# A hybrid RG-LRU and Conformer block on one core: four dot products of a gate at another place in the queue, and a layer norm taken about a mean of seven tiles

## The chip, the cores and the metric

The kernel runs on one core of a Trainium2 chip. The metric is the device time of one execution in microseconds (us); several executions are timed and their median is given. A core has five engines that take their instructions from queues of their own, each strictly in its order: TensorE (PE, matmuls), VectorE (DVE), ScalarE (ACT), GpSimd (POOL) and SyncE (SP, which only starts transfers here). They wait for each other by semaphores.

## The reference, cut to what matters

Two layers, a latent stream of 1024 tokens by 1024 features. Each layer is a mixer and then a gated ConvFFN; each of the two is scaled and shifted by six vectors (shift, scale, gate, twice) that come from the conditioning vector `c`. What the change touches is the second gate `g2` of the first layer, and the layer norm inside the second layer's mixer.

```
s_c = silu(c)
mod = s_c @ ada_w[i] + ada_b[i]                      # 6 x 1024 values
sh1, sc1, g1, sh2, sc2, g2 = split(mod, 6)
...
def conv_ffn(xm, w_up, cw, cb, w_down, rows, width):
    u = dwconv2d(xm @ w_up, cw, cb, rows, width)     # 3x3 depthwise, 5632 channels
    v, g = split(u, 2)
    return (silu(g) * v) @ w_down
h = h + g2 * conv_ffn(xm2, ...)

def conformer_conv(xm, w1, b1, cw, cb, lng, lnb, w2, b2):
    u = xm @ w1 + b1
    a, g = split(u, 2)
    v = dwconv1d(a * sigmoid(g), cw, cb, (15, 15))   # 31 taps
    v = silu(layernorm(v, lng, lnb))
    return v @ w2 + b2
def layernorm(x, g, b):
    mu = mean(x); var = mean(square(x - mu))
    return (x - mu) * rsqrt(var + EPS) * g + b
```

## The kernel before, in words

Activations lie with features on the 128 partitions (8 tiles of 128 features) and tokens along the free dimension, in two halves of 512 tokens (half 0, half 1). Every large product is made of three fp32r products (high by high, low by high, high by low), for which weights and activations are split: ACT copies the high part, POOL or DVE subtracts it (`whi`, `wlo` for weights, `xmh`, `xml` for activations, `zh`, `zl` and `dnh`, `dnl` in the FFN). PE's accumulators are four tiles `P[0]` to `P[3]` of two banks each (the rows call them `ps`).

**Who sets the order.** The class `Order` keeps a clock of estimated durations. `o.pe(...)` puts a PE step at the place where the code stands; the steps of the other engines wait in a pool, and the one with the earliest possible start, then the lowest `prio`, then the oldest, is issued next. So `prio` and the estimated readiness set each engine's fixed queue; on the chip an engine takes its rows in that order and waits wherever a row isn't ready.

**The FFN of layer 0** (`ffn`, 22 pairs p). A pair makes two tiles of the up projection (`col_tile`, f = p and 22 + p), each in one of `P[0]`, `P[1]`, `P[2]` in turn. ACT and DVE make the 3x3 convolution of a tile from PSUM (`ffn_conv`: one ACT step, eight DVE steps, which are called taps below, into `cv`), ACT takes the SiLU, DVE multiplies (`cv<-cv,cv`), and ACT and POOL split the product (`zh`, `zl`). From pair 3 on, `between()` puts a step of the down projection (`unit`) after every fourth k-step: 12 matmuls into `P[3]`, then on DVE `h<-ps,mod,h`, which multiplies by the gate `g2` and adds to the residual. The next unit needs `P[3]` free again.

**The gate's dots.** `g2` of layer 0 is eight columns of `mod` (q = 40 to 47), each a dot of a 128x1024 weight tile with `sC` (silu(c) on all partitions) by `ada_dot`: four on DVE (`raw,mod<-raw,sC`), made in `first_tiles` of pair 0 with `prio=3`, then four on POOL (`raw<-raw,sC`) with the sum on ACT (`raw,mod<-raw`). The tiles are loaded into a ring of two buffers, `raw_76` and `raw_77`, which the down projection's weights (`down_in`) share. `ada_bias(0, 5)` adds the bias to the eight columns (`mod<-mod,vec`); every `h` step needs it.

**The Conformer** (`conformer`). The 31-tap convolution of tiles 0, 2, 4, 6 is done on DVE (`taps`, into `CV`), that of tiles 1, 3, 5, 7 on PE (`conv`, 36 steps of three 256-column matmuls each into `P[3]`, four groups j of nine shifts). After a PE tile DVE copies its two halves to `yt`, two transfers write them to DRAM (`cdr<-yt`), four read them back rearranged (`sC<-cdr`), and ACT adds the bias (`CV<-sC,vec`). Tile 7 is the last. POOL has meanwhile summed tiles 0 to 4 into `lna` (`nacc`).

**The layer norm before.** `center(0)` multiplies `lna` and tiles 5, 6, 7 by a matrix of 1/1024 (`ones`), which gives the mean on all partitions; DVE subtracts it from eight tiles (`CV<-CV,ps`), ACT squares each, PE sums the squares with `ones` into `P[1]`, ACT and DVE make the reciprocal root (`rs`). `src` then feeds the second product (`k_outer`, 8 steps k per half): for each tile DVE multiplies by `rs`, ACT takes SiLU and the high part, DVE the low part (`xml<-CV,xmh`). In step k=0 PE also makes the mean of half 1 (`center(1)`), and in step k=3 it makes half 1's variance (`deviation`) from the sum of squares that DVE and POOL add up in turn (`nacc<-nacc,tt`).

Of the kernel before, what the change touches and what calls it, by code (L numbers as in the profile page):

```python
# [13 lines left out]
AF = mybir.ActivationFunctionType  # L14
ALU = mybir.AluOpType
ADD, SUB, MULT = ALU.add, ALU.subtract, ALU.mult
# [5 lines left out]
ND = D // P  # L22
# [258 lines left out]
class Net:  # L281
# [115 lines left out]
    def split(self, raw, rawB, slot, eng="pool", n=1024, hi_eng="act"):  # L397
        hi, lo, hB, lB = slot
        if hi_eng == "act":
            self.act(n, hi, raw, AF.Copy, [rawB], [hB])  # L400
        else:
            self.o.op("dve", 0.1 + n * 0.00053, lambda: self.nc.vector.tensor_copy(hi, raw), [rawB], [hB])
        self.tten(n, lo, raw, hi.bitcast(F32), SUB, [rawB, hB], [lB], eng=eng)
# [136 lines left out]

    def ada_dot(self, l, q, eng="dve", after=(), prio=0):

        t, b = self.load_raw(self.a["ada"][l, q], after=() if prio else after)
        col, mB = self.mod[l][:, q:q + 1], self.modB[l][q // 8]
        if eng == "dve":
            self.stt(1024, t, t, 1.0, self.sC, MULT, MULT, [b, self.sCB], [b], [mB], accum=col, after=after, prio=prio)
        else:
            self.tten(1024, t, t, self.sC, MULT, [b, self.sCB], [b], eng=eng, prio=prio)  # L550
            self.act(1024, t, t, AF.Copy, [b], [b], [mB], accum=col)
# [511 lines left out]
    def ffn(self, l, end, last=None):  # L1063
        o = self.o
# [39 lines left out]
        def quarter(g, q):  # L1104
            quarters[g, q] = load_down(g, q * 256, 256, dn.next())
# [12 lines left out]
        def zsplit(p, a, aB):  # L1118
            zh, zl, zhB, zlB = zr.next()
            Z[p] = zh, zl, [[zhB, zlB]] * 2  # L1120
            self.act(1024, zh, a, AF.Copy, [aB], [zhB])
            self.tten(1024, zl, a, zh.bitcast(F32), SUB, [aB, zhB], [zlB], eng="pool")
# [16 lines left out]
        ada = [(0, q) for q in range(40, 48)] + [(1, q) for q in range(48)] if l == 0 else []  # L1139
# [4 lines left out]
        for p in range(NF):  # L1144
            if p >= 3 and p % 2 == 1 and p < NF - 1:
                g = (p - 3) // 2
                todo += [(g, q, d) for q in range(4) for d in (2 * q, 2 * q + 1)]
            pts, accs = [], []
            if ada and 0 < p < 3:
                for _ in range(2):  # L1150
                    self.ada_dot(*ada.pop(0), "pool", prio=3)
                if p == 2:
                    self.ada_bias(0, 5)
            for q in ((), (0,), (1, 2))[p] if p < 3 else ():
                quarter(0, q)
            if p == 0:
                self.first_tiles((0, 1), lambda ops: [self.ada_dot(*ada.pop(0), prio=3, after=ops) for _ in range(4)] if ada else None)
                pts, nt = [0, 1], 2
            for i, f in enumerate((p, NF + p)):
                if p:  # L1160
                    self.col_tile(self.w_next(), nt % 3, between)
                    pts.append(nt % 3)
                    nt += 1
                acc, accB = cv.next()
                accs.append((acc, accB))
                if f < 2 * NF - 1:
                    self.ffn_conv(l, f, pts[i], acc, accB)
            (a, aB), (gt, gB) = accs
            if p < NF - 1:
                self.act(1024, gt, gt, AF.Silu, [gB], [gB])  # L1170
                self.tten(1024, a, a, gt, MULT, [aB, gB], [aB])
                zsplit(p, a, aB)
            else:
                last_gate(2 * NF - 1, pts[1], a, aB, gt, gB)
            for _ in range(3 if p > 2 else 0):
                if ada:
                    self.ada_dot(*ada.pop(0), "pool", prio=3)

        if l == 0:
# [4 lines left out]
            m = self.mod[1][:, 16:24]  # L1184
# [24 lines left out]
    def conformer(self, pool):  # L1209
        nc, o = self.nc, self.o  # L1210
        W, HS = 1024, 4
        CV = pool.tile([P, ND, W], F32, name="CV")
        cvB = [[Buf(), Buf()] for _ in range(ND)]
# [10 lines left out]
        yt, yB = pool.tile([P, W], F32, name="yt"), [Buf(), Buf()]  # L1224
        yr, yrB = self.sC, Buf(after=[self.sCB])
        rs2 = [self.rs, (pool.tile([P, 512], F32, name="rs2"), Buf())]
        lna = self.acc
        LATE = (5, 6, 7)
# [4 lines left out]
        outB = [[Buf(), Buf()] for _ in range(ND)]  # L1233
# [32 lines left out]
        def glu(m, pt):  # L1266
# [12 lines left out]
            self.act(W, inner(hi), split(xr), AF.Copy, [xrB], [hB], prio=-2)  # L1279
            self.tten(W, inner(lo), split(xr), inner(hi).bitcast(F32), SUB, [xrB, hB], [lB], prio=-2)  # L1280

        def conv(m):
            hi, lo, hB, lB = xs[m // 2 % 2]
            out = self.P[3].rearrange("p a (b s) -> p (a b) s", b=2)
            slot = None
            for j in range(4):
                for n, d in enumerate(SHIFTS):
                    i = j * len(SHIFTS) + n
                    if i % 8 == 0:
                        slot = self.w_next()  # L1290
                    wh, wl, whB, wlB = slot
                    c, s = slice(i % 8 * P, i % 8 * P + P), slice(HS + d, HS + d + 256)

                    def go():
                        for q, (w, x) in enumerate(((wh, hi), (wh, lo), (wl, hi))):
                            self.mm(out[:, j, :], w[:, c], x[:, j, s], n == 0 and q == 0, n == len(SHIFTS) - 1 and q == 2)

                    o.pe(3 * (256 / 2400 + 0.011), go, [whB, wlB, hB, lB], [self.PB[3][j // 2]])
            for h in range(2):
                c = slice(512 * h, 512 * h + 512)  # L1300
                self.ts(512, yt[:, c], self.P[3][:, h, :], 1.0, None, MULT, None, [self.PB[3][h]], [yB[h]], prio=-2)
                self.dma(self.cdr[m][:, c], yt[:, c], 262144, r=[yB[h]], w=[outB[m][h]], prio=-2)
            src = self.cdr[m].rearrange("(o c) (j s) -> j c o s", o=4, j=4)
            yrB.begin()
            for j in range(4):
                self.dma(split(yr)[32 * j:32 * j + 32], src[j], 131072, r=[outB[m][j // 2]], wp=[yrB], prio=-2)

            for h in range(2):
                c = CV[:, m, h * 512:h * 512 + 512]
                self.act(  # L1310
                    512, c.rearrange("p (s i) -> p s i", i=4), split(yr)[:, :, 128 * h:128 * h + 128].rearrange("p i s -> p s i"),
                    AF.Identity, [yrB], [cvB[m][h]], bias=self.v("cf_conv_b", m), prio=-1,
                )
            summed(m)
# [18 lines left out]
        def center(h, bank, sums):  # L1333

            xs = [(CV[:, m, h * 512:h * 512 + 512], cvB[m][h]) for m in range(ND)]
            parts = [lna[h], *(xs[m] for m in LATE)]
            mu, muB = self.P[bank[0]][:, bank[1], :], self.PB[bank[0]][bank[1]]
            for i, (t, tB) in enumerate(parts):
                o.pe(0.87, lambda: self.mm(mu, self.ones, t, i == 0, i == len(LATE)), [self.onesB, tB], [muB])
            for x, b in xs:  # L1340
                self.tten(512, x, x, mu, SUB, [b, muB], [b], prio=3 * h - 2)
            for m in range(ND):
                sums(m, *xs[m])

        var = self.P[1][:, 0, :]

        def sums(m, x, b):
            sq, sqB = self.tt.next()
            self.act(512, sq, x, AF.Square, [b], [sqB])
            o.pe(0.87, lambda: self.mm(var, self.ones, sq, m == 0, m == ND - 1), [self.onesB, sqB], [self.PB[1][0]])  # L1350

        center(0, (0, 0), sums)
        self.rsqrt(512, rs2[0][0], var, [self.PB[1][0]], [rs2[0][1]])

        def deviation(bank):
            ms = self.stat(*lna[1], bank)
# [2 lines left out]
        first = {0: lambda bank: center(1, bank, lambda m, x, b: self.norm_add(m, 1, x, b, ("dve", "pool")[m % 2])), 3: deviation}  # L1359
# [4 lines left out]
        def src(hf, k):  # L1364
            while self.fed < min(hf * ND + k + 5, 16):
                h, m = order[self.fed]
                self.fed += 1
                c = slice(h * 512, h * 512 + 512)
                x, b = CV[:, m, c], cvB[m][h]
                self.tten(512, x, x, rs2[h][0], MULT, [b, rs2[h][1]], [b])  # L1370
                silu = self.act(512, x, x, AF.Silu, [b], [b], bias=self.v("cf_ln_b", m), scale=self.v("cf_ln_g", m))
                self.z_split(m, x, b, "dve")
                if self.fed == 16:
                    self.sqrt_soon([silu])
            return self.z_slot((hf * ND + k) % 8)
# [81 lines left out]
```

## Time and profile before

| | us |
|---|---|
| median of 3 runs | 2440.19 (2438.97 to 2441.34) |
| the profiled execution, its own time | 2438.16 |
| its span from the first to the last instruction | 2436.4 |
| PE busy | 2326.2 (95%) |
| DVE busy | 1896.6 (78%) |
| ACT busy | 967.3 (40%) |
| POOL busy | 798.1 (33%) |
| PE idle for others, longest single wait | 23.0 |

The share of an engine is an average over stages. What a place is worth is read from PE's idle time at that place and from what released PE there. A number in square brackets at the end of a row is the engine's idle time just before that row, with the instruction that ended it.

### The profile page before, as it was taken

Reading aid. Unit: us, or ns where it says so; the run is one execution under the profiler, and the core shown is the slowest. Engines: PE = TensorE matmul, PEld = TensorE weight load, DVE = VectorE, ACT = ScalarE, POOL = GpSimd, SP = SyncE. Lnnn points to the kernel's source line nnn. Section 1 sums busy time; section 2 is a strip of 40 time slices with the busy share of each in tenths; the row PEclk is TensorE's granted clock in tenths of the full one; section 3 lists DMA queues with packets and bytes.
Section 4 is the critical chain, followed back from the end, with each engine's and each line's share of the span. In section 5 each row is a group of like instructions: output and inputs, shape, how many; then the busy total and the mean of one; then the engine's idle time right before and its main releaser. Section 6 shows DMA issues by size and latency. Waiting matters only on the chain.

```text
span 2436.4 us, 26124 instructions
## 1 busy us (share of the span) xinstructions
PE 2326.2 (95%) x10440; PEld 1892.8 (78%) x10440; DVE 1896.6 (78%) x1752; ACT 967.3 (40%) x1141; POOL 798.1 (33%) x409
## 2 busy tenths in 40 slices
PE   7999999889789999999999999889999999999997
PEld 2788888667578888888887888667888888888886
DVE  6677877776867777777878898677997777777878
ACT  4577777544233333333324333365322221222223
POOL 1100000354345544554523233245333322332323
PEclk9999999899899999999999999899999999999999
DMA  6324325253132323223211233422111111111101
GB/s 262 120 84 144 94 84 162 96 198 117 55 101 95 104 87 104 95 88 103 91 35 36 66 114 105 138 70 91 52 58 52 44 39 52 52 52 48 44 26 70
DMA packets 82442, 214.98 MB, mean 88 GB/s; under 512 B 8528, under 2 KB 33104, under 8 KB 82192
## 3 DMA queue, kind: packets, MB, share of 16 engines
q1 hardware_dynamic: 80448, 210.68, 26.3%
q10 hardware_dynamic: 1872, 2.62, 0.3%
q8 instruction: 82, 1.34, 0.2%
q14 instruction: 40, 0.33, 0.0%
HBM read 192.10 MB, written 13.63 MB: 84 GB/s over the span
## 4 chain that ended last, share of the span: by engine, by line
PE 70%; DVE 16%; ACT 5%; issue 3%; DMA 2%; POOL 2%; SPq 0%; ACTq 0%; DVEq 0%; POOLq 0%
PE ps L441 70%; DVE cv L362 4%; DVE CV L362 3%; DVE F L770 1%; ACT F L354 1%; POOL wlo L369 1%; DVE F L362 1%; DVE tt L362 1%; DVE F L369 1%; DVE rs L384 1%; ACT tt L354 1%; DVE raw L362 1%; ACT L354 1%; DVE h L362 1%; ACT whi L354 1%
## 5 line engine op out<-in xcount | busy, mean ns | idle before, releaser
L362 DVE SCALAR_TENSOR_TENSOR cv<-ps,vec,cv 128x960 f32<-128x960 f32 (+2 forms) x720 | 861.5, 1198 | 203.6 <-ACT cv L354 185.2
L441 PE MATMUL ps<-xmh,whi 128*128 128x512 f32 x2272 | 744.5, 394 | 19.7 <-ACT xmh L354 8.9
L441 PE MATMUL ps<-xmh,wlo 128*128 128x512 f32 x2272 | 738.0, 392 | 9.5 <-POOL wlo L369 5.9
L441 PE MATMUL ps<-xml,whi 128*128 128x512 f32 x2272 | 740.5, 393 | 4.6 <-DVE xml L362 4.2
L369 POOL TENSOR_TENSOR wlo<-wraw,whi 128x1024 fp32r<-128x1024 f32 (+1 forms) x164 | 399.8, 2442 | 712.6 <-ACT whi L354 694.9
L441 PEld LDWEIGHTS ps<-xmh,whi 128*128 128x128 f32 x2272 | 427.8, 189 | 115.9 <-ACT xmh L354 12.0
L441 PEld LDWEIGHTS ps<-xmh,wlo 128*128 128x128 f32 x2272 | 429.4, 189 | 103.1 <-POOL wlo L369 7.9
L441 PEld LDWEIGHTS ps<-xml,whi 128*128 128x128 f32 x2272 | 429.8, 189 | 102.4 <-DVE xml L362 9.4
L362 DVE SCALAR_TENSOR_TENSOR h<-ps,mod,h 128x1024 f32<-128x1024 f32 (+2 forms) x216 | 231.5, 1080 | 61.0 <-PE ps L441 60.8
L354 ACT ACTIVATE whi<-wraw 128x1024 fp32r<-128x1024 f32 (+1 forms) x198 | 205.2, 1042 | 123.3 <-PE ps L441 51.5
L354 ACT ACTIVATE cv<-ps,vec 128x1024 f32<-128x1024 f32 (+1 forms) x90 | 105.9, 1181 | 299.5 <-PE ps L441 280.5
L369 POOL TENSOR_TENSOR zl<-cv,zh 128x1024 fp32r<-128x1024 f32 x42 | 101.2, 2411 | 350.6 <-ACT zh L354 350.6
L441 PE MATMUL ps<-zh,dnh 128*128 128x512 f32 x576 | 180.1, 393 | 23.0 <-DVE h L362 23.0
L369 POOL TENSOR_TENSOR raw<-raw,sC 128x1024 f32<-128x1024 f32 x52 | 125.1, 2406 | 178.7 <-DMA raw<-ada_in 174.0
L441 PE MATMUL ps<-zl,dnh 128*128 128x512 f32 x576 | 181.4, 397 | 0.0
L441 PE MATMUL ps<-zh,dnl 128*128 128x512 f32 x576 | 177.8, 390 | 0.0
L354 ACT ACTIVATE raw<-raw 128x1024 f32<-128x1024 f32 x52 | 55.2, 1062 | 289.4 <-POOL raw L369 289.4
L354 ACT ACTIVATE cv<-cv 128x1024 f32<-128x1024 f32 (+1 forms) x46 | 47.0, 1022 | 293.5 <-DVE cv L362 293.3
L369 POOL TENSOR_TENSOR dnl<-raw,dnh 128x512 fp32r<-128x512 f32 x72 | 94.0, 1307 | 202.5 <-ACT dnh L354 202.5
L362 DVE SCALAR_TENSOR_TENSOR CV<-ps,vec,CV 128x1009 f32<-128x1009 f32 (+14 forms) x120 | 153.1, 1275 | 8.6 <-ACT CV L354 4.9
L441 PEld LDWEIGHTS ps<-zh,dnh 128*128 128x128 f32 x576 | 108.6, 189 | 45.9 <-DVE h L362 23.4
L441 PEld LDWEIGHTS ps<-zh,dnl 128*128 128x128 f32 x576 | 108.4, 188 | 26.4
(141 smaller groups left out, 2414.6 us busy)
## 6 DMA issues: line engine op xcount, KB each, us to landing
raw<-ada_in SPq DMA_DIRECT2D x88, 512.0 KB, 4.2
wraw<-up_in SPq DMA_DIRECT2D x88, 512.0 KB, 3.3
raw<-down_in SPq DMA_DIRECT2D x72, 256.0 KB, 3.2
wraw<-w_in SPq DMA_DIRECT2D x32, 512.0 KB, 3.3
wraw<-w_in_in SPq DMA_DIRECT2D x20, 512.0 KB, 3.9
wraw<-w_out_in SPq DMA_DIRECT2D x20, 512.0 KB, 3.7
wraw<-cw_in SPq DMA_DIRECT2D x16, 512.0 KB, 3.6
wraw<-gw_in SPq DMA_DIRECT2D x10, 512.0 KB, 3.4
```

What stands on the lines that cost most here:

```text
L354: "act", 0.21 + n * 0.00083, lambda: self.nc.scalar.activation(out, in_, func, **kw),
L362: lambda: self.nc.vector.scalar_tensor_tensor(out=out, in0=in0, scalar=scalar, in1=in1, op0=op0, op1=op1, **kw),
L369: return self.o.op(eng, dur, lambda: e.tensor_tensor(out=out, in0=in0, in1=in1, op=op), r, w, wp, prio=prio)
L384: return self.o.op("dve", 0.07 + n * 0.0063, lambda: self.nc.vector.reciprocal(out=out, in_=in_), r, w)
L441: self.nc.tensor.matmul(out, w, x, start=start, stop=stop)
L770: lambda t=t, a=a, ig=ig, rev=rev: nc.vector.tensor_tensor_scan(rev(t), rev(a), rev(ig), 0.0, op0=MULT, op1=ADD),
```

## The change

It has two parts that don't touch each other. **First**, the four DVE dots of `g2` get priority 0 in place of 3, the same as the taps of the convolution. `early` keeps the load's old rule (it doesn't wait for `after`).

**Second**, half 0's layer norm. `provisional()` is called inside the last convolution tile, after the sixth shift of its last group, and multiplies `lna` and tiles 5 and 6 by `ones` into `P[0]`'s second bank: the sum of seven tiles over 1024. `deviate` subtracts 8/7 of it, which is the mean of the seven tiles, from each tile (one DVE step, PSUM and SBUF in) and squares it on ACT. Tiles 0 to 6 and their sums of squares no longer need tile 7. When tile 7 is there, its deviation goes to a buffer `w` (`raw_76`), one product of `w` with `ones` gives `mu`, the distance of the true mean from the provisional one (the seven tiles' deviations sum to nothing), the variance is the mean square less `mu` squared, and `d`, a copy of `mu` in SBUF, is subtracted from each tile before it is multiplied by `rs`.

```diff
-    def ada_dot(self, l, q, eng="dve", after=(), prio=0):
+    def ada_dot(self, l, q, eng="dve", after=(), prio=0, early=False):
-        t, b = self.load_raw(self.a["ada"][l, q], after=() if prio else after)
+        t, b = self.load_raw(self.a["ada"][l, q], after=() if early else after)
...
-                self.first_tiles((0, 1), lambda ops: [self.ada_dot(*ada.pop(0), prio=3, after=ops) for _ in range(4)] if ada else None)
+                self.first_tiles((0, 1), lambda ops: [self.ada_dot(*ada.pop(0), early=True, after=ops) for _ in range(4)] if ada else None)
...
+        def provisional():
+            parts = [lna[0], *((CV[:, m, :512], cvB[m][0]) for m in LATE[:-1])]
+            for i, (t, tB) in enumerate(parts):
+                o.pe(0.87, lambda: self.mm(self.P[0][:, 1, :], self.ones, t, i == 0, i == len(parts) - 1), [self.onesB, tB], [self.PB[0][1]])
...
+                    if m == ND - 1 and j == 3 and n == 5:
+                        provisional()
...
-        def sums(m, x, b):
-            sq, sqB = self.tt.next()
-            self.act(512, sq, x, AF.Square, [b], [sqB])
-            o.pe(0.87, lambda: self.mm(var, self.ones, sq, m == 0, m == ND - 1), [self.onesB, sqB], [self.PB[1][0]])
-        center(0, (0, 0), sums)
-        self.rsqrt(512, rs2[0][0], var, [self.PB[1][0]], [rs2[0][1]])
+        def deviate(m, y, yB):
+            self.stt(512, y, mp, -ND / (ND - 1.0), CV[:, m, :512], MULT, ADD, [cvB[m][0], mpB], [yB], prio=-3)
+            sq, sqB = self.tt.next()
+            self.act(512, sq, y, AF.Square, [yB], [sqB], prio=-4)
+            return sq, sqB
+        for m in range(ND - 1):
+            total(var, varB, *deviate(m, CV[:, m, :512], cvB[m][0]), m == 0, False)
+        w, wB = vt[:, :512], vB
+        sq = deviate(ND - 1, w, wB)
+        total(mu, muB, w, wB, True, True)
+        total(var, varB, *sq, False, True)
+        sq, sqB = self.tt.next()
+        self.act(512, sq, mu, AF.Square, [muB], [sqB], prio=-4)
+        self.act(512, d, mu, AF.Copy, [muB], [dB], prio=-3)
+        self.tten(512, r, var, sq, SUB, [varB, sqB], [rB], prio=-4)
+        self.rsqrt(512, r, r, [rB], [rB])
+        inverse = list(rB.w)
...
+                if h == 0:
+                    x, b = (w, wB) if m == ND - 1 else (x, b)
+                    o.op("dve", 0.72, lambda x=x: nc.vector.tensor_tensor(out=x, in0=x, in1=d, op=SUB), [b, dB], [b], after=inverse if m else ())
                 self.tten(512, x, x, rs2[h][0], MULT, [b, rs2[h][1]], [b])
```

DVE's queue at the start of layer 0's FFN, the place of the fourth dot (`raw_77,mod`; `cv_3479` is the convolution of pair 0's first tile):

```order
 L362 SCALAR_TENSOR_TENSOR raw_76,mod_92<-raw_76,sC 128x1024
 L362 SCALAR_TENSOR_TENSOR cv_3479<-ps_65,vec,cv_3479 128x960 x2
+L362 SCALAR_TENSOR_TENSOR raw_77,mod_92<-raw_77,sC 128x1024
 L362 SCALAR_TENSOR_TENSOR cv_3479<-ps_65,vec,cv_3479 128x16x63 x2
 L362 SCALAR_TENSOR_TENSOR cv_3479<-ps_65,vec,cv_3479 128x15x63 x4
```

The fourth dot has moved from behind the taps of pair 2's second tile (five tiles' taps later) to behind the second tap of the first tile; the bias step `mod<-mod,vec` now stands behind the second tap of pair 1's first tile (`cv_3481`), and the first `h` step behind the seventh tap of pair 2's first tile (`cv_3480`), where before it came after the dot and the bias.

PE's queue in the last convolution tile (`cxh`, `cxl`: its input, `whi_82`, `wlo_83`: its weights), the first and the last row of each piece of the difference:

```order
 L441 MATMUL ps_68<-cxl_7759,whi_82 128x256
 L441 MATMUL ps_68<-cxh_7758,wlo_83 128x256
+L441 MATMUL ps_65<-nacc_89,ones 128x512
+L441 MATMUL ps_65<-CV,ones 128x512 x2
 L441 MATMUL ps_68<-cxh_7758,whi_82 128x256
-L441 MATMUL ps_65<-nacc_89,ones 128x512
-L441 MATMUL ps_65<-CV,ones 128x512 x3
-L441 MATMUL ps_66<-tt,ones 128x512 x8
+L441 MATMUL ps_66<-tt,ones 128x512 x7
+L441 MATMUL ps_65<-raw_76,ones 128x512
+L441 MATMUL ps_66<-tt,ones 128x512
```

The mean's products have moved into the tile, three matmul steps of three ahead of its end; the squares of seven tiles, the product of `w` and the last square follow the tile.

DVE's queue from the copies of the last tile on, before (-) and now (+):

```order
-L377 TENSOR_SCALAR yt<-ps_68 128x512 x2
-L369 TENSOR_TENSOR CV<-CV,ps_65 128x512 x8
+L377 TENSOR_SCALAR yt<-ps_68 128x512
+L362 SCALAR_TENSOR_TENSOR CV<-ps_65,CV 128x512
+L377 TENSOR_SCALAR yt<-ps_68 128x512
+L362 SCALAR_TENSOR_TENSOR CV<-ps_65,CV 128x512 x6
+L362 SCALAR_TENSOR_TENSOR raw_76<-ps_65,CV 128x512
+L369 TENSOR_TENSOR rs<-ps_66,tt 128x512
+L1397 TENSOR_TENSOR CV<-CV,nacc_89 128x512
 L384 RECIPROCAL rs<-rs 128x512
```

A deviation stands between the two copies; the subtraction of `d` from tile 0 stands ahead of the reciprocal, and seven more of these (L1397, both inputs in SBUF) follow it, one ahead of each tile's product with `rs`. In ACT's queue the copy of a weight tile (`whi<-wraw`) stands between the last square and the square of `mu`.

## Rows read from the trace of the kernel before

**Rows 1.** PE's costliest wait over the span: for whom, us in total, times, longest.
```profile
PE ps L441 <- DVE h L362: 26.5, 4, 23.0
```

**Rows 2.** PE in time, layer 0's FFN: start, us, engine, line, form.
```profile
606.58 0.70 PE L441 MATMUL ps<-xmh,whi 128*128 128x512 f32 x2 [0.21 <-DVE cv L362]
...
644.78 0.62 PE L441 MATMUL ps<-zh,dnh 128*128 128x512 f32 x2
...
647.54 0.62 PE L441 MATMUL ps<-xmh,whi 128*128 128x512 f32 x2
...
652.54 0.61 PE L441 MATMUL ps<-xmh,wlo 128*128 128x512 f32 x2
676.15 1.22 PE L441 MATMUL ps<-zh,dnh 128*128 128x512 f32 x2 [23.00 <-DVE h L362]
...
680.83 0.62 PE L441 MATMUL ps<-xmh,whi 128*128 128x512 f32 x2
```

**Rows 3.** DVE in time, the same stretch.
```profile
596.41 21.08 DVE L362 SCALAR_TENSOR_TENSOR cv<-ps,vec,cv 128x960 f32<-128x960 f32 x17
617.50 1.23 DVE L369 TENSOR_TENSOR cv<-cv,cv 128x1024 f32<-128x1024 f32 x1
...
638.54 1.23 DVE L369 TENSOR_TENSOR cv<-cv,cv 128x1024 f32<-128x1024 f32 x1
...
658.30 1.22 DVE L362 SCALAR_TENSOR_TENSOR raw<-raw,sC 128x1024 f32<-128x1024 f32 x1
...
674.54 0.17 DVE L369 TENSOR_TENSOR mod<-mod,vec 128x8 f32<-128x8 f32 x1 [13.75 <-ACT raw L354]
674.82 1.28 DVE L362 SCALAR_TENSOR_TENSOR h<-ps,mod,h 128x1024 f32<-128x1024 f32 x1
```

**Rows 4.** POOL and ACT in time, the same stretch.
```profile
598.18 2.40 POOL L369 TENSOR_TENSOR wlo<-wraw,whi 128x1024 fp32r<-128x1024 f32 x1 [7.89 <-ACT whi L354]
...
617.37 1.04 ACT L354 ACTIVATE raw<-raw 128x1024 f32<-128x1024 f32 x1
```

**Rows 5.** PE in time, the end of the convolution and half 0's norm.
```profile
1561.45 1.02 PE L441 MATMUL ps<-nacc,ones 128*128 128x512 f32 x2
1562.31 1.88 PE L441 MATMUL ps<-CV,ones 128*128 128x512 f32 x4
1570.94 2.07 PE L441 MATMUL ps<-CV,ones 128*128 128x512 f32 x2 [6.75 <-ACT CV L354]
...
1589.64 0.79 PE L441 MATMUL ps<-xmh,whi 128*128 128x512 f32 x1 [6.40 <-ACT xmh L354]
...
1612.26 1.12 PE L441 MATMUL ps<-nacc,ones 128*128 128x512 f32 x2 [1.88 <-POOL nacc L369]
```

**Rows 6.** DVE, POOL and ACT in time, the same stretch.
```profile
1561.65 1.29 DVE L377 TENSOR_SCALAR yt<-ps 128x512 f32<-128x512 f32 x2 [1.57 <-PE ps L441]
...
1584.00 3.35 DVE L384 RECIPROCAL rs<-rs 128x512 f32<-128x512 f32 x1 [6.08 <-ACT rs L354]
...
1598.14 1.88 DVE L369 TENSOR_TENSOR CV<-CV,ps 128x512 f32<-128x512 f32 x3 [2.36 <-PE ps L441]
...
1601.82 2.88 DVE L369 TENSOR_TENSOR nacc<-nacc,tt 128x512 f32<-128x512 f32 x1
...
1608.61 1.27 DVE L369 TENSOR_TENSOR xml<-CV,xmh 128x512 fp32r<-128x512 f32 x1
...
1601.75 2.40 POOL L369 TENSOR_TENSOR wlo<-wraw,whi 128x1024 fp32r<-128x1024 f32 x1
...
1608.03 1.30 POOL L369 TENSOR_TENSOR nacc<-nacc,tt 128x512 f32<-128x512 f32 x1 [1.90 <-DVE nacc L369]
...
1569.72 2.24 ACT L354 ACTIVATE CV<-sC,vec 128x512 f32<-128x512 f32 x2 [5.55 <-DMA sC<-cdr]
```

**Rows 7.** Busy time by window: PE, PEld, DVE, ACT, POOL, granted clock, DMA share.
```profile
750.00:1000.00 250.00, 250.00 (x1097) 205.73 (x1096) 192.96 (x161) 80.65 (x104) 128.24 (x62) 1.00 0.30 99
...
640.00:700.00 60.00, 37.00 (x155) 29.99 (x154) 37.77 (x34) 14.88 (x19) 24.79 (x12) 0.80 0.20 66
```

More of the change, by code (lines that the diff above doesn't have):

```diff
@@ L1343, in center, with total @@
                 sums(m, *xs[m])
-        var = self.P[1][:, 0, :]
-        def sums(m, x, b):
-            sq, sqB = self.tt.next()
-            self.act(512, sq, x, AF.Square, [b], [sqB])
-            o.pe(0.87, lambda: self.mm(var, self.ones, sq, m == 0, m == ND - 1), [self.onesB, sqB], [self.PB[1][0]])
-        center(0, (0, 0), sums)
-        self.rsqrt(512, rs2[0][0], var, [self.PB[1][0]], [rs2[0][1]])
+        r, rB = rs2[0]
+        d, dB = lna[0]
+        (mp, mpB), (mu, muB), (var, varB) = [(self.P[i][:, j, :], self.PB[i][j]) for i, j in ((0, 1), (0, 0), (1, 0))]
+        def total(out, outB, t, tB, first, last):
+            o.pe(0.87, lambda: self.mm(out, self.ones, t, first, last), [self.onesB, tB], [outB])
+        def deviate(m, y, yB):
+            self.stt(512, y, mp, -ND / (ND - 1.0), CV[:, m, :512], MULT, ADD, [cvB[m][0], mpB], [yB], prio=-3)
+            sq, sqB = self.tt.next()
+            self.act(512, sq, y, AF.Square, [yB], [sqB], prio=-4)
[12 more added lines that the diff above has]
+        inverse = list(rB.w)
         def deviation(bank):
```

## The prediction

> **What bounds the kernel now.** Start with the busy time by window [rows 7]: from 750 to 1000 us PE is busy for 250 of 250 us and DVE for 193. In the FFN's steady state PE is the bound, so a stall of PE there is not made up later. From 640 to 700 PE is busy for only 37 of 60. PE's waits [rows 1] name it: it waited 26.5 us in all for `h` on DVE, 23.0 of that at once. PE in time [rows 2] shows the place: the second down-projection unit starts at 676.15 instead of at 652.54 + 0.61 = 653.15. DVE in the same stretch [rows 3] shows why. The fourth dot of the gate runs only at 658.30, behind five tiles' taps; its buffer is free at 659.5, and then two POOL dots have to go through that buffer one after the other; the bias step comes at 674.54, 15.0 us later, and the first `h` at 674.82. DVE stood idle for 13.75 us of it. The second place is half 0's layer norm [rows 5]: the convolution ends at 1561.45, and the first matmul of the next product starts at 1589.64, 28.2 us later, in which PE has only the ones-products.
>
> **First part: the dots.** Nothing is added; the fourth dot moves to behind two taps of the first tile.
>
> *Removed:* the stall, −23.0 [rows 2]. After it PE ran slowly: that unit took 680.83 − 676.15 = 4.68 us against 647.54 − 644.78 = 2.76 for the unit before, so −1.9 more. [...]
>
> *Added:* a tap takes 21.08 / 17 = 1.24, so the dot's turn is at 596.41 + 2 × 1.24 = 598.9. POOL then runs a `wlo` subtraction, 598.18 to 600.58 [rows 4]. The dot reads two tensors in SBUF. A DVE step of that kind beside a `wlo` is in the trace [rows 6]: the sum `nacc<-nacc,tt` at 1601.82 took 2.88 and ended at 1604.70, 0.55 after POOL's 1601.75 + 2.40 = 1604.15. On its own it takes 0.68 (the sums of that form without a POOL step beside them), so it did nothing until about 0.13 before POOL's end. By that row the dot works from 600.45 and, at 1.22 [rows 3], ends at 601.7: DVE is 2.8 late, and at least 1.2 if nothing holds it. The delay reaches PE in full: the tile at 606.58 already waited 0.21 for those taps [rows 2]. I take 2.8.
>
> [...] Another row does not agree: the two `xml` steps at 1608.61 took 1.27 together, undisturbed, beside a POOL sum of 1608.03 to 1609.33 [rows 6], so I don't charge every overlap with it.
>
> A wait of 2.8 may cost PE some clock: none after the wait of 1.88 at 1612.26, 1.9 after that of 23.0; I take 0.7, with 0 and 1.5 as bounds.
>
> *Where the stall goes.* What is late next is the bias step. Its two POOL dots in `raw_77` start 601.7 and need the 15.0 us that the trace shows for that chain, so 616.7 at the earliest; ACT's queue puts their sums behind pair 0's SiLU, which moves from 617.5 to 620.3 with the taps, and two sums of 1.2 end at 622.7. DVE's turn for the bias: 617.50 + 2.8, a product of 1.23 and a tap of 1.24 further, 622.8. No wait is left over, and no margin. DVE has nothing to spare there (its taps for a tile end about 0.8 before PE needs its bank), so each us by which the bias comes later costs about one. The first `h` follows the seventh tap of pair 2's first tile: 638.54 + 2.8 + 1.2 + 6 × 1.24 = 650, done at 651.3; PE's second unit comes at 653.15 + 2.8 = 656. That wait is gone with 4.7 to spare.
>
> First part: −23.0 − 1.9 + 2.8 + 0.7 = −21.4; bounds −23.7 (the dot not held, no clock lost) and −17 (the clock's 1.5, and the bias 3 late).
>
> **Second part: the layer norm.** *Up to the first matmul.* The provisional products take what the same three take now, 1561.45 to 1562.31 + 1.88 = 1564.19, 2.7 us, and lie inside the tile, so the tile ends at 1564.2. Both `yt` copies come after the tile's end (1561.65, after 1.57 idle for PE, though the first copies groups that were done long before), and one deviation of about 0.66 now stands between them: the second ends at 1564.4 + 0.6 + 0.66 + 0.68 = 1566.3 instead of 1562.94. The way through DRAM takes 1569.72 − 1562.94 = 6.8 [rows 6], so tile 7 reaches ACT at 1573.1, 3.4 later than now. Six more deviations, seven squares and seven products of 0.86 lie beside that way. Then: two halves of tile 7 on ACT (2.24, 1575.3; the deviation lies beside the second), the square (1575.95), a `whi` copy that stands next in ACT's queue (1577.0), square and copy of `mu` (1578.2), the variance on DVE (1578.3), then the subtraction of `d` from tile 0. That one reads two SBUF tensors, and POOL takes up its `wlo` as soon as the `whi` copy is done, 1577.1 to 1579.5; by the row at 1601.82 the subtraction ends at 1580.0, and the reciprocal is queued behind it. It starts at 1580.0 instead of 1584.00. From its end to PE it is 1589.64 − 1587.35 = 2.3 as now. So PE starts 4.0 sooner; 4.9 without that hold, 3.0 if the way through DRAM takes 1 more, since a weight load now stands between the two writes in SP's queue.
>
> *From there to half 1's variance.* PE makes half 1's mean early in k=0; DVE's first subtraction of it (1598.14) starts 8.5 after PE's start, after 2.36 of idle time. Four of the seven other subtractions of `d` fit ahead of it, into that idle time. Three of 0.65 lie between 1598.14 and the sum of squares that PE waits for at 1612.26, 14.1 later; PE waited 1.88 for it, so it has no slack to give. Worked through in the new order without any hold by POOL, the variance comes 15.9 after the first subtraction; with the one hold of 2.2 that the row shows, 18.1; with every overlap of two-input steps and POOL's four steps there, 19.1. I take 18.0, nearest to the row: +3.9, bounds 1.8 and 5.0. PE's wait then is 5.8. After the 6.40 at 1589.64 PE spent its first 9 steps at 0.43 apart where it later takes 0.23, after the 1.88 none; I take 1.0, bounds 0 and 2.5.
>
> Second part: −4.0 + 3.9 + 1.0 = +0.9; bounds −3.1 and +4.5. The eight subtractions take back what the shorter chain gives.
>
> **Sum.** −21.4 + 0.9 = −20.5. The profiled execution took 2438.16, its span 2436.4 and 1.8 around it; that is 2.0 under the median of the runs, 2440.19. On the median the sum gives 2419.7.
>
> **The rivals.** *The norm gains as well:* DVE's steps slip past POOL's, the dot at 598.9 and the subtractions too. Speaks for it: the pair at 1608.61. Against: 1601.82, and DVE's load in that stretch. Dots −23.7, norm −3.1: 2413.4.
>
> [...]
>
> *Part of the stall stays at the bias step.* For it: the margin is nothing, and three loads of 512 KB are asked for within 3 us on one queue. Against: 616.7 against 622.8. Five to ten us late would give 2425 to 2430.
>
> *Slower than before:* DVE, whose queue is strict, stands in front of the bias step while the taps behind it are ready. Before, DVE had no tap to do at that point; now it has. It costs what the sums come late, one for one; from 25.4 on it is slower than before by more than 0.2%, so only if the chain of two dots took 46 us instead of 15. About 2446 at 27 late.
>
> *The change doesn't do what it says:* `h` is late for another reason than the dot. The bias waited for ACT's sums of exactly that buffer, so I give it little; the time would be about 2441.
>
> **How the numbers follow.** Forecast 0.50 (own range 2416 to 2423), the norm gains as well 0.20, the rule to the letter 0.12 (it lies in the forecast's range), part of the stall stays 0.13, no effect 0.02, slower 0.03. A range from 2412 to 2427 takes in the first three and the lower part of the fourth. A difference under 0.2% (4.9 us) can't be told from none: faster 0.95, within it 0.02, slower 0.03.
>
> **What would show it.** PE's wait of 23.0 gone, and the tile that waited 0.21 now waiting about 3; the dot about 2.8 long; a wait at the bias step under 1. In the norm: tile 7 on ACT about 3.4 later after the convolution's products than now, PE's start 24 after 1561.45's place instead of 28.2, and its wait for the sum of squares near 6 instead of 1.88. Wrong if PE stands at the second unit again, or if that last wait stays at 2.

## The result, and the profile after

The changed kernel takes 2425.33 us (median of 4 runs, 2421.27 to 2427.6) against 2439.58 before in the same comparison: a ratio of 0.994, 95% interval 0.9923 to 0.9958, a fall of 14.3 where 20.5 was forecast. The forecast was 2419.7 with a range of 2412 to 2427; its own likeliest range, 2416 to 2423, was missed by 2.3. The profiled execution took 2425.06 (span 2423.3), 13.1 less than the one before.

PE's waits over the span, the rows that answer to [rows 1]: the 23.0 for `h` is gone (what is left are three short waits, the longest 2.3), and a wait of 6.0 for `nacc` has come, which was 1.88 [rows 5].

```profile
PE ps L441 <- POOL nacc L369: 6.0, 1, 6.0
...
PE ps L441 <- DVE h L362: 3.5, 3, 2.3
```

DVE, then POOL, then PE in time at the start of layer 0's FFN, after. They answer to [rows 2 to 4].

```profile
597.66 2.47 DVE L362 SCALAR_TENSOR_TENSOR cv<-ps,vec,cv 128x960 f32<-128x960 f32 x2
600.05 2.89 DVE L362 SCALAR_TENSOR_TENSOR raw<-raw,sC 128x1024 f32<-128x1024 f32 x1
...
623.70 0.16 DVE L369 TENSOR_TENSOR mod<-mod,vec 128x8 f32<-128x8 f32 x1
...
653.28 1.28 DVE L362 SCALAR_TENSOR_TENSOR h<-ps,mod,h 128x1024 f32<-128x1024 f32 x1 [2.15 <-PE ps L441]
...
599.45 2.39 POOL L369 TENSOR_TENSOR wlo<-wraw,whi 128x1024 fp32r<-128x1024 f32 x1 [7.92 <-ACT whi L354]
601.80 3.40 POOL L369 TENSOR_TENSOR raw<-raw,sC 128x1024 f32<-128x1024 f32 x1
...
610.52 1.10 PE L441 MATMUL ps<-xmh,whi 128*128 128x512 f32 x2 [2.86 <-ACT dnh L354]
```

The fourth dot starts at 600.05 while POOL's subtraction runs until 601.84. It takes 2.89 instead of 1.22 and ends 1.1 after POOL. PE's tile behind it waits 2.86, where it waited 0.21. (The row puts this down to ACT's `dnh`, which ends at 610.46; DVE's six taps behind the dot end at about 602.86 + 6 × 1.24 = 610.3, and in e3, told below, the same wait of 2.87 is put down to DVE's `cv`.) The bias step has no idle time in front of it, and at the first `h` DVE now waits for PE, not PE for DVE.

PE in time at half 0's norm, and the clock of the stretch behind the wait, by window (columns as in [rows 7]).

```profile
1569.70 0.80 PE L441 MATMUL ps<-xmh,whi 128*128 128x512 f32 x1 [7.23 <-ACT xmh L354]
...
1595.67 2.08 PE L441 MATMUL ps<-nacc,ones 128*128 128x512 f32 x2 [6.03 <-POOL nacc L369]
1596.76 1.42 PE L441 MATMUL ps<-xmh,whi 128*128 128x512 f32 x1
1597.97 0.63 PE L441 MATMUL ps<-xml,whi 128*128 128x512 f32 x1
...
1600.52 0.40 PE L441 MATMUL ps<-xml,whi 128*128 128x512 f32 x1
...
1595.60:1605.00 9.40, 9.33 (x29) 6.89 (x30) 4.05 (x2) 3.05 (x4) 1.51 (x2) 0.74 0.00 0
```

After the wait of 6.03 PE works at half clock (0.43 from one matmul to the next instead of 0.23) until 1600.5, which is 4.85 us; the granted clock is 0.50 from 1595.67 to 1600.50, 1.00 from there to 1605.00, and 0.74 in the whole window. Half clock and full clock stand below for these two spacings (for a pair of matmuls about 0.86 and about 0.46).

To see where the time went, the span is cut at PE rows that every profile has. These are the borders: of before, those not yet shown (1589.64 and 1612.26 stand in [rows 5]), then of after, those not yet shown.

```profile
582.29 0.50 PE L441 MATMUL ps<-xmh,whi 128*128 128x512 f32 x1 [0.22 <-ACT xmh L354]
1327.62 0.51 PE L441 MATMUL ps<-xml,whi 128*128 128x512 f32 x1 [0.23 <-DVE xml L362]
1546.14 0.36 PE L441 MATMUL ps<-cxh,whi 128*128 128x256 f32 x1 [2.28 <-DVE yt L377]
1649.34 1.13 PE L441 MATMUL ps<-nacc,ones 128*128 128x512 f32 x2 [0.57 <-DVE nacc L369]
```

```profile
583.53 0.50 PE L441 MATMUL ps<-xmh,whi 128*128 128x512 f32 x1 [0.22 <-ACT xmh L354]
1308.07 0.50 PE L441 MATMUL ps<-xml,whi 128*128 128x512 f32 x1 [0.25 <-DVE xml L362]
1528.37 0.36 PE L441 MATMUL ps<-cxh,whi 128*128 128x256 f32 x1 [2.49 <-DVE yt L377]
1635.76 1.12 PE L441 MATMUL ps<-nacc,ones 128*128 128x512 f32 x2 [1.06 <-DVE nacc L369]
```

Differences of their starts, in us, for all profiles of this study (the experiments are told below). The columns: to the FFN of layer 0; the FFN; the Conformer's first product and convolution up to its last tile; from there to the first matmul of the second product; from there to half 1's variance; from there to the next norm's sum; the rest of the span.

| profile | start | FFN | conv | tile 7 to product | to variance | to next norm | rest |
|---|---|---|---|---|---|---|---|
| before | 582.29 | 745.33 | 218.52 | 43.50 | 22.62 | 37.08 | 787.06 |
| after | 583.53 | 724.54 | 220.30 | 41.33 | 25.97 | 40.09 | 787.54 |
| e1 dots only | 580.48 | 722.92 | 219.08 | 44.21 | 22.73 | 37.14 | 787.04 |
| e2 norm only | 580.83 | 745.15 | 218.62 | 41.16 | 26.03 | 40.23 | 788.58 |
| e3 after again | 581.15 | 722.94 | 219.41 | 39.77 | 27.17 | 40.72 | 786.74 |
| e4 distance in PSUM | 579.64 | 722.92 | 219.25 | 39.59 | 26.67 | 39.52 | 786.81 |
| e5 no subtractions | 583.56 | 724.52 | 219.99 | 40.96 | 22.08 | 37.04 | 788.45 |
| e6 three on POOL | 579.94 | 722.91 | 219.50 | 40.57 | 22.71 | 37.11 | 786.96 |
| e7 dot at tap 4 | 580.30 | 723.26 | 218.27 | 44.22 | 22.96 | 37.87 | 788.32 |
| e8 e6 and e7 | 580.81 | 723.20 | 218.86 | 40.08 | 22.99 | 37.12 | 787.04 |
| e9 dot at tap 6 | 582.18 | 721.19 | 219.86 | 44.92 | 22.85 | 37.95 | 788.65 |
| e10 best | 582.38 | 721.27 | 220.41 | 40.81 | 23.10 | 37.18 | 786.95 |

After less before, stage by stage: +1.2, −20.8, +1.8, −2.2, +3.4, +3.0, +0.5. The first, third and last stages have the same work in every kernel, and they scatter by 3.9, 2.1 and 1.9 from profile to profile.

### The profile page after: what moved, and what is told of

It reads as the page before. It is cut to its first block, busy times and chain, and to the rows that moved or that the text cites. A ratio compares the mean times of both kernels' runs of the same rounds, so it can differ in the third digit from the quotient of the medians.

```text
span 2423.3 us, 26137 instructions
## 1 busy us (share of the span) xinstructions
PE 2330.2 (96%) x10440; PEld 1895.2 (78%) x10440; DVE 1902.7 (79%) x1761; ACT 968.0 (40%) x1143; POOL 799.2 (33%) x409
## 4 chain that ended last, share of the span: by engine, by line
PE 74%; DVE 14%; ACT 4%; DMA 2%; issue 2%; POOL 1%; SPq 0%; ACTq 0%; DVEq 0%; POOLq 0%
PE ps L441 74%; DVE CV L362 2%; DVE F L770 1%; ACT F L354 1%; DVE cv L362 1%; DVE F L362 1%; DVE tt L362 1%; DVE rs L384 1%; DVE F L369 1%; POOL wlo L369 1%; ACT L354 1%; ACT tt L354 1%; DVE raw L362 1%; DVE xml L362 1%; DVE h L362 1%
## 5 line engine op out<-in xcount | busy, mean ns | idle before, releaser
L441 PEld LDWEIGHTS ps<-xmh,whi 128*128 128x128 f32 x2272 | 429.1, 190 | 122.8 <-ACT xmh L354 13.1
L369 POOL TENSOR_TENSOR zl<-cv,zh 128x1024 fp32r<-128x1024 f32 x42 | 101.3, 2412 | 340.8 <-ACT zh L354 340.8
L369 POOL TENSOR_TENSOR raw<-raw,sC 128x1024 f32<-128x1024 f32 x52 | 126.2, 2427 | 155.8 <-DMA raw<-ada_in 154.7
L441 PEld LDWEIGHTS ps<-zl,dnh 128*128 128x128 f32 x576 | 108.1, 188 | 24.4
```

The lines of the kernel that those rows point to most:

```text
L369: return self.o.op(eng, dur, lambda: e.tensor_tensor(out=out, in0=in0, in1=in1, op=op), r, w, wp, prio=prio)
L441: self.nc.tensor.matmul(out, w, x, start=start, stop=stop)
```

## The experiments

Theory: the first part does what was forecast, and the second costs more than forecast, through the DVE steps it adds and the clock behind the wait they cause. Rival: the shortfall is the scatter of single executions, and the norm is worth its +0.9.

**e1, the first part alone.** The norm is that of before.

```diff
-self.ada_dot(*ada.pop(0), prio=3, after=ops)
+self.ada_dot(*ada.pop(0), early=True, after=ops)
```

> The first part alone, the layer norm as before. Theory (the norm is what took back the gain): of the 5.6 us by which the changed kernel is slower than the sum of the prediction, most lies in the second part, so this kernel runs at 2439.6 - 20.8 = 2418.8, some 5 to 6 us faster than both parts together (2425.3). The trace has no PE wait over 5 us between 1540 and 1660 except the four that the kernel before has there. Rival (the shortfall is the clock of single executions, and the norm is worth the +0.9 of the prediction): 2424 to 2425, within 1.5 us of both parts together.

2417.61 (5 runs, 2415.47 to 2423.3), ratio 0.991 (0.9897 to 0.9924): near the theory's 2418.8 and not the rival's 2424. PE's wait for the sum of squares is 1.89 and full clock follows it:

```profile
1589.42 1.13 PE L441 MATMUL ps<-nacc,ones 128*128 128x512 f32 x2 [1.89 <-POOL nacc L369]
1589.98 0.79 PE L441 MATMUL ps<-xmh,whi 128*128 128x512 f32 x1
1590.61 0.40 PE L441 MATMUL ps<-xml,whi 128*128 128x512 f32 x1
...
1592.00 0.39 PE L441 MATMUL ps<-xml,whi 128*128 128x512 f32 x1
...
1589.40:1599.00 9.60, 9.58 (x40) 7.62 (x41) 6.82 (x3) 6.71 (x8) 4.01 (x2) 1.00 0.06 12
```

The same matmul (the eighth behind the sum) starts 2.58 after the sum here and 1600.52 − 1595.67 = 4.85 after it with both parts: the half clock costs 2.3.

**e2, the second part alone** (the dots at priority 3).

> The second part alone, the dots at priority 3 as before. Theory: 4 to 6 us slower than before, 2444 to 2446, with PE's wait for half 1's sum of squares at 6.0 as in both parts together. Rival: within 1.5 us of before, 2439 to 2441.

2443.18 (11 runs), ratio 1.0012 (1.0003 to 1.0021): slower by 2.9, less than the theory's 4 to 6 and more than the rival's 1.5. The wait is 6.02.

**e3, the changed kernel again.**

> The changed kernel once more, for a second profile. Theory: 2425 as before, and the trace again has the wait of 6.0 for half 1's sum of squares with the matmuls behind it at half clock for 4 to 5 us. Rival (clock of single executions): the slow matmuls behind that wait are gone or stand elsewhere, and the median falls to 2421 or below.

2421.06 (5 runs, 2418.97 to 2425.75), ratio 0.9926 (0.9912 to 0.9939). The median is the rival's, the trace the theory's: the wait is 6.06, and the two stages behind the product's start are even longer than in the first profile (27.17 and 40.72, where they were 25.97 and 40.09). So the norm's cost is there in both profiles of this program, and a part of the 5.6 by which it lay above the forecast was scatter. Two rows differ from the first profile of the same program. The tile behind the dot now goes on at full clock after the same wait, and the subtraction from tile 0 stands beside POOL's `wlo` (1554.83 to 1557.18), takes 1.85 and holds the reciprocal up:

```profile
608.12 0.70 PE L441 MATMUL ps<-xmh,whi 128*128 128x512 f32 x2 [2.87 <-DVE cv L362]
...
1554.83 2.35 POOL L369 TENSOR_TENSOR wlo<-wraw,whi 128x1024 fp32r<-128x1024 f32 x1 [10.68 <-ACT whi L354]
...
1555.87 1.85 DVE L1397 TENSOR_TENSOR CV<-CV,nacc 128x512 f32<-128x512 f32 x1
1557.64 3.34 DVE L384 RECIPROCAL rs<-rs 128x512 f32<-128x512 f32 x1
```

**e4, the distance read from PSUM.**

```diff
-... [... ((0, 1), (0, 0), (1, 0))]
+... [... ((0, 1), (3, 0), (1, 0))]
-self.act(512, d, mu, AF.Copy, [muB], [dB], prio=-3)
-o.op(... nc.vector.tensor_tensor(out=x, in0=x, in1=d, op=SUB), [b, dB], ...)
+o.op(... nc.vector.tensor_tensor(out=x, in0=x, in1=mu, op=SUB), [b, muB], ...)
```

> Both parts, but the distance of the means stays in PSUM (bank P[3][0] in place of P[0][0]) and the eight subtractions read it there; the copy on ACT falls away. Theory (two of the subtractions were held by POOL because both their inputs lay in SBUF: 1.78 and 1.75 long against 0.68): no subtraction takes over 0.8, the sum of squares comes 2.2 earlier, PE's wait falls from 6.0 to about 3.8, and the time by 2.2 to 3.5 to 2422 to 2423. Rival (the delay is the number of DVE steps, whichever memory they read): subtractions 0.7, but the wait stays above 5 and the time at 2425.

2419.15 (5 runs), ratio 0.9916 (0.9903 to 0.9929), below the theory's 2422. No subtraction takes over 0.69, so the two holds were POOL's. But the wait only falls to 4.29, not to 3.8, and half clock still follows (0.42 to 0.43 from one matmul to the next). The hold has in part moved one step on: the product with `rs` behind each of the two subtractions, whose inputs both lie in SBUF, now meets the same POOL step and takes 1.07, where it took 0.69. And the new place made a wait of its own: the distance lies in one bank of `P[3]`, half 1's mean in the other, and the fifth subtraction and the mean's products now wait for each other. That the shared tile is the reason was not tried apart.

```profile
1568.77 0.69 DVE L1395 TENSOR_TENSOR CV<-CV,ps 128x512 f32<-128x512 f32 x1 [3.28 <-PE ps L441]
...
1569.51 1.98 PE L441 MATMUL ps<-CV,ones 128*128 128x512 f32 x4 [0.78 <-DVE CV L1395]
...
1578.38 1.61 POOL L369 TENSOR_TENSOR nacc<-nacc,tt 128x512 f32<-128x512 f32 x1 [0.70 <-DVE nacc L369]
...
1579.47 1.07 DVE L369 TENSOR_TENSOR CV<-CV,rs 128x512 f32<-128x512 f32 x1
...
1588.07 1.99 PE L441 MATMUL ps<-nacc,ones 128*128 128x512 f32 x2 [4.29 <-POOL nacc L369]
```

**e5, the eight subtractions left out.**

```diff
-o.op("dve", 0.72, lambda x=x: nc.vector.tensor_tensor(out=x, in0=x, in1=d, op=SUB), ...)
```

> Both parts, without the eight subtractions of d (half 0 is then normalised about the mean of seven tiles instead of eight: that part of the computation is left out). Theory (the norm's loss is the eight DVE steps and the clock after the wait they cause): PE's wait for half 1's sum of squares falls from 6.0 to 1.9 or less, the matmuls behind it run at full clock, the last tile's start to the next product stays at 39 to 41 (43.5 before), and the time is 2413 to 2415, 3 to 5 below the dots alone (2417.6). Rival (half 1's chain is late because PE starts sooner, not because DVE has more to do): the wait stays above 4 and the time at 2418 or more.

2416.6 (4 runs, 2413.99 to 2418.89), ratio 0.9904 (0.9889 to 0.9918): above the theory's 2415 and below the rival's 2418, but the trace answers the question. The wait is back at 1.89, the stages behind the product's start at 22.08 and 37.04, although PE starts the product as early as in the changed kernel. The subtractions, not the earlier start, made the wait, and the half clock came with the wait (here it is 0.22 to 0.24 from one matmul to the next).

```profile
1591.11 1.12 PE L441 MATMUL ps<-nacc,ones 128*128 128x512 f32 x2 [1.89 <-POOL nacc L369]
```

**e6, three subtractions on POOL.** Tiles 5, 6 and 7, written right behind the copy of `d`; the other five stay.

```diff
+for x, b in [(CV[:, m, :512], cvB[m][0]) for m in (5, 6)] + [(w, wB)]:
+    self.tten(512, x, x, d, SUB, [b, dB], [b], eng="pool", prio=-4)
```

> Both parts, with the subtractions of tiles 5, 6 and 7 given to POOL, which has nothing to do for 16 us there; the other five stay on DVE. Theory: POOL does the three in about 4 us beside DVE's reciprocal, DVE's steps ahead of the sum of squares fall by three (2.0) and by the two holds (2.2), PE's wait falls to 1.9 to 2.5 with no slow matmuls behind it, time 2414 to 2416. Rival (POOL's three steps hold DVE's two-input steps in turn): a multiplication by rs or the subtraction of tile 0 takes 1.8 or more, PE starts later by as much, and the time is 2419 or more.

2415.38 (4 runs, 2411.49 to 2417.03), ratio 0.9897 (0.9883 to 0.9911). POOL does the three in 1556.65 to 1560.81, beside the reciprocal; the wait is 1.89 and full clock follows it (0.22 to 0.24). The subtraction of tile 0 takes 1.85 as in e3, held by the `wlo` that was there before, not by the moved steps.

```profile
1556.65 2.94 POOL L369 TENSOR_TENSOR CV<-CV,nacc 128x512 f32<-128x512 f32 x2
1559.55 1.26 POOL L369 TENSOR_TENSOR raw<-raw,nacc 128x512 f32<-128x512 f32 x1
...
1557.16 3.34 DVE L384 RECIPROCAL rs<-rs 128x512 f32<-128x512 f32 x1
...
1585.63 1.13 PE L441 MATMUL ps<-nacc,ones 128*128 128x512 f32 x2 [1.89 <-POOL nacc L369]
```

**e7, the dot behind the fourth tap** (first part alone). The load stays where it was; the dot is made after the tile's taps and depends on tap 4.

```diff
+self.stt(1024, t, t, 1.0, self.sC, MULT, MULT, ..., accum=self.mod[0][:, q:q + 1], after=[taps[3]], prio=-1)
```

> The first part alone, with the fourth dot behind the fourth tap instead of the second, where POOL's subtraction has ended. Theory (POOL held the dot): the dot takes 1.2 instead of 2.9, PE's wait at the tile behind falls from 2.9 to 1.2, and the time by 1.6 against the dots alone, to 2416. Rival (the dot is slow because its load lands late, or PE waits for another step): the dot or the wait stays at 2.9, and the time at 2417.6.

2418.27 (5 runs), ratio 0.9912 (0.9899 to 0.9924); the dot takes 3.21 and PE's wait is 3.22. That is the rival's number, but not its reason: POOL runs its own dot just there.

```profile
599.18 2.40 POOL L369 TENSOR_TENSOR raw<-raw,sC 128x1024 f32<-128x1024 f32 x1 [0.56 <-DMA raw<-ada_in]
...
599.44 3.21 DVE L362 SCALAR_TENSOR_TENSOR raw<-raw,sC 128x1024 f32<-128x1024 f32 x1
```

**e8, e6 and e7 together.**

> The last two together: both parts, three subtractions on POOL, the fourth dot behind the fourth tap. Theory: the gains add, 2412.5 to 2414.5, below both kernels. Rival: POOL's steps cost DVE what they take from it, 2417 or more.

2417.38 (5 runs, 2411.98 to 2419.49), ratio 0.9906 (0.989 to 0.9922). The norm's stages are those of e6 (40.08, 22.99, 37.12), the FFN's those of e7. The theory's 2412.5 to 2414.5 was missed: as e7 brought nothing, there was nothing to add up. The median is the rival's, but the stages do not bear out its reason, as the norm is as short as in e6.

**e9, the dot behind the sixth tap** (first part alone; `taps[5]`).

> The first part alone, the fourth dot behind the sixth tap. In the run with the fourth tap the dot stood beside POOL's own dot (599.18 to 601.58) and took 3.2; between that one and POOL's next subtraction (603.79) there is room. Theory (a two-input DVE step that starts while POOL works on SBUF is held to POOL's end): the dot takes 1.2, PE's wait at the tile behind falls from 2.9 or 3.2 to 1.2 to 1.5, and the stage from the FFN's start to the Conformer's becomes 1.5 shorter (721.4 for 722.9). Rival (the dot is long for another reason, such as its buffer's load): still 2.9 or more, stage 722.9.

The dot takes 1.22 between two POOL steps, PE's wait is 1.14, and the stage is 721.19, 1.7 shorter than e1's 722.92, as the theory had it.

```profile
600.76 2.41 POOL L369 TENSOR_TENSOR raw<-raw,sC 128x1024 f32<-128x1024 f32 x1 [0.26 <-DMA raw<-ada_in]
...
603.71 1.22 DVE L362 SCALAR_TENSOR_TENSOR raw<-raw,sC 128x1024 f32<-128x1024 f32 x1
...
605.39 2.37 POOL L369 TENSOR_TENSOR wlo<-wraw,whi 128x1024 fp32r<-128x1024 f32 x1 [2.22 <-ACT whi L354]
...
607.43 0.70 PE L441 MATMUL ps<-xmh,whi 128*128 128x512 f32 x2 [1.14 <-DVE cv L362]
```

The median, 2418.93 (4 runs), ratio 0.9911 (0.9894 to 0.9927), doesn't show it: 1.7 is less than what the unchanged stages scatter.

**e10, all of it.** e6 and e9, tile 0's subtraction read from PSUM (`P[0]`), and both `yt` copies of tile 7 ahead of the first deviation.

> Both parts in the best form so far: the dot behind the sixth tap, three subtractions on POOL, tile 0's subtraction reading the distance from PSUM, and both copies of tile 7 ahead of the first deviation. Theory: the subtraction of tile 0 takes 0.7 instead of 1.85 and the reciprocal starts up to 0.5 sooner, the way through DRAM 0.6 sooner, the dot 1.5 shorter; with three subtractions on POOL at 2415.4 that makes 2412.5 to 2413.5. Rival (nothing of it is on the path): the stage from the last tile to half 1's end stays at 100.2 to 100.4 and the time at 2415.

2413.29 (4 runs, 2411.95 to 2413.91), ratio 0.9893 (0.9878 to 0.9907): the lowest median, clear of both kernels. Its interval overlaps with those of e1 and e6, but in the same comparison its four runs all lie below e9's four (2414.75 to 2419.38). The norm's three stages sum to 101.1, in e6 to 100.4. Tile 0's subtraction takes 0.69, but the reciprocal starts 34.98 after the last tile's start, in e6 34.81: it now waits 0.79 for ACT's root, which comes 1.1 later than in e6 (34.23 for 33.16 after the last tile's start). So the last two edits together brought nothing; why the root is later was not tried. What e10 gains over the dots alone stands in the stages of e6 and e9.

## Why the prediction was right, and where it was off

**The dots: right.** The stall and its slow unit are gone, the dot is held by POOL (2.89 for the 2.8 forecast), the bias step finds no wait and `h` is not late. The FFN's stage is 745.33 before and 722.9 in four of the six profiles with this dot, −22.4, and 724.5 in the other two, −20.8. Those two differ in the clock after the wait of 2.9: in the first profile of the changed kernel the two matmuls at 610.52 take 1.10, in e3 at 608.12 they take 0.70. The forecast of −21.4 held 0.7 for it, between the 0 and the 1.6 that it turned out to be. (The far bound of this part, −17, adds up to −17.6 by its own terms.)

The dot is 2.73 to 3.21 long in the eight profiles in which a POOL step came first, ends 1.1 after that step in each, and is 1.22 in e9; POOL's own dot at 601.80, which came second, takes 3.40 instead of 2.40. The prediction set one row against a hold at every overlap, the step at 1608.61, and misread it: the row counts one step, not two [rows 6]. It is 1.27 long instead of 0.68 and ends 0.55 after POOL's sum (1609.33), so it was held like the others, and it spoke for no rival. In the rows read here no DVE step with two SBUF inputs that began with more than 0.2 of a POOL step to go escaped the hold.

**The norm's way to the product: right but for 0.5.** The way through DRAM took 0.7 more than before (1549.63 to 1557.13 on ACT), which the forecast had among its bounds. The stage is 41.33, 41.16 and 39.77 in the three profiles of this norm and 43.5 to 44.9 in the four of the old one; the means differ by 3.5, forecast 4.0. The hold of tile 0's subtraction, which the forecast charged with 0.9, came in e3 alone (1.85; 0.68 in the other two), and e3's stage is nevertheless the shortest: the scatter here is larger than that term.

**The wait for half 1's sum: right, in part by luck.** The sum came 18.3 after DVE's first subtraction of half 1 (1577.41), forecast 18.0; PE waits 6.03, forecast 5.8. But the one hold of 2.2 that the forecast counted, of the sum `nacc<-nacc,tt`, did not come. Three others did: a product with `rs` of 1.66 and two subtractions of `d`, 1.78 and 1.75 long, each beside a POOL sum.

```profile
1577.41 1.28 DVE L369 TENSOR_TENSOR CV<-CV,ps 128x512 f32<-128x512 f32 x2 [1.69 <-PE ps L441]
...
1579.94 1.66 DVE L369 TENSOR_TENSOR CV<-CV,rs 128x512 f32<-128x512 f32 x1
...
1584.95 1.78 DVE L1397 TENSOR_TENSOR CV<-CV,nacc 128x512 f32<-128x512 f32 x1
...
1589.78 1.75 DVE L1397 TENSOR_TENSOR raw<-raw,nacc 128x512 f32<-128x512 f32 x1
...
1579.44 1.61 POOL L369 TENSOR_TENSOR nacc<-nacc,tt 128x512 f32<-128x512 f32 x1 [16.17 <-ACT tt L354]
...
1584.58 1.60 POOL L369 TENSOR_TENSOR nacc<-nacc,tt 128x512 f32<-128x512 f32 x1 [0.70 <-DVE nacc L369]
...
1589.57 1.40 POOL L369 TENSOR_TENSOR nacc<-nacc,tt 128x512 f32<-128x512 f32 x1 [3.39 <-ACT tt L354]
```

Against 0.68 to 0.69 alone these are 3.2 in all, 1.0 more than forecast; the way without holds was 15.1 instead of 15.9, and the two errors nearly cancel.

**The clock behind that wait: the term that was too small.** The prediction says "I take 1.0, bounds 0 and 2.5". It cost 2.3 in the first profile and in e2, and 2.9 in e3, where three more matmuls are slow. The stage is 40.1 to 40.7 with this norm and 37.1 to 38.0 with the old one; the means differ by 2.8. The next wait, 1.06 instead of 0.57, is not the norm's alone: e7 and e9, with the old norm and full clock, have 1.04 there.

```profile
1628.95 1.12 PE L441 MATMUL ps<-nacc,ones 128*128 128x512 f32 x2 [1.04 <-DVE nacc L369]
```

The nearest row had the size: 9 steps at 0.43 instead of 0.23 after the wait of 6.40 are 1.8. I took the middle between a short wait without a loss and this one, though the forecast wait was as long as this one. With 2.3 to 2.8 in its place the second part is +2.2 to +2.7, and +3.0 is what the three stages give as the difference of those means (−3.5, +3.6 and +2.8); e2 measured +2.9, e3 less e1 +3.45. A hold at every overlap ("the rule to the letter" in the prediction's chances) would have been nearer: with the variance at 19.1 (+5.0) and the bound of 2.5 for the clock it makes −4.0 + 5.0 + 2.5 = +3.5. Its wait of 1.88 + 5.0 = 6.9 is too long although the three holds cost the 3.2 that it charges (19.1 less 15.9): its error lies in the 15.9, not in an overlap that went free.

**What of the 5.6 is left.** The norm accounts for 2, the dots of this profile for 0.6 (−20.8 for −21.4). The rest lies in stages whose code is the same: in the profile +1.2 at the start and +1.8 in the convolution. Of the latter 1.5 is clock: PE works at half clock behind a wait of 1.26 (0.85 to 0.90 from one pair to the next instead of 0.46, until 1450.2; the granted clock is 0.52 from 1446.71 to 1450.20, in the same stretch of before, 1466.31 to 1469.80, it is 1.00). In the other eleven profiles the same wait costs no clock. The first row is of before, the others of after:

```profile
1466.31 0.73 PE L441 MATMUL ps<-xmh,wlo 128*128 128x512 f32 x2 [1.27 <-POOL wlo L369]
...
1446.71 1.10 PE L441 MATMUL ps<-xmh,wlo 128*128 128x512 f32 x2 [1.26 <-POOL wlo L369]
1447.61 1.05 PE L441 MATMUL ps<-xmh,whi 128*128 128x512 f32 x2
```

The second comparison of the same program gave 2421.06. The dots alone take 2417.61, so the second part as it stands costs about 3 rather than giving anything. What sets the scatter of the unchanged stages was not tried.

## What to carry to other kernels

A step that shortens one chain by adding work to an engine moves the wait to the next thing that this engine feeds: price the added steps at the place where PE waits for that engine next, and with the wait the clock that PE loses behind it (here 2.3 to 2.9 after 6.0), taken from a wait of the same length in the trace. Give such steps to an engine that stands idle (with three of the eight on POOL the norm's loss of 3 became a gain by its stages: they sum to 100.2, 100.4 and 101.1 in e8, e6 and e10, and to 103.2 to 105.7 with the old norm; of the medians only e10's, against e9, shows it clear of the scatter), and look in the trace which POOL step runs at the moment in which a two-input DVE step will start (the dot took 2.73 to 3.21 beside one, 1.22 between two). When the gain is smaller than the scatter of unchanged stages, compare the stage and not the median.

## What the runs showed of the hardware

The time for which a DVE step was held by POOL stood in its own duration, not in the idle time before it: 1.22 became 2.89, 0.68 became 1.85, and no wait is named; so did that of POOL's dot at 601.80, where 2.40 became 3.40. The end of these holds lay at a fixed distance: at the FFN's start and in the norm, in all twelve profiles, each single DVE step with two SBUF inputs that began while a POOL step had more than 0.2 to go ended 0.54 to 0.56 after that step if it was 128x512, and 1.07 to 1.10 after it if it was 128x1024. Whether the steps met changed from one execution to the next: tile 0's subtraction began 2.25 after POOL's `wlo` in the first profile of the changed kernel and took 0.68; in the second it began 1.04 after it and took 1.85.

After the same wait of 2.9 PE went on at full clock in four profiles (a pair of matmuls every 0.45 to 0.54) and at half clock in two (every 0.84 to 0.94), and after 3.2 at full clock in e7 and e8; ahead of half 1's variance it kept its clock after 1.9 in each of eight profiles (0.22 to 0.24 from one matmul to the next), and lost it after 4.3 and 6.0 in each of four (0.40 to 0.43). A wait of 1.26 in the convolution cost clock in one of twelve. So in these profiles a wait of 1.26 or of 2.9 had no one price in clock.
